# A decoder trunk on one core: the even mixer's projections in another order, ScalarE's order written out there, and the next norm finished on VectorE

## The chip, the cores and the metric

One core of one Trainium2 chip. The metric is the device time of one execution in microseconds. The kernel before has three timed runs of 955.73, 953.67 and 952.62 us; their median, 953.67 us, is what the change is held against. One further execution was profiled.

## The reference

Two layers over a sequence of 256 tokens with 1024 channels, everything in float32. Each layer is an FFN, a mixer, and another FFN, each behind an RMS norm and added to the residual x. Layer 0 has the even mixer, layer 1 the odd one. Cut to what matters:

```python
def swiglu(x, w_gate, w_up, w_down):
    return (jax.nn.silu(x @ w_gate) * (x @ w_up)) @ w_down

def even_mixer(h, ...):
    a_val, a_gate, q, k, v = jnp.split(h @ w_in, cuts, axis=-1)   # 512, 512, 512, 128, 128
    u = a_val * jax.nn.sigmoid(a_gate)
    u = causal depthwise convolution of u, 31 taps, + conv_b
    u = jax.nn.silu(layer_norm(u, ln_g, ln_b))
    q = rms_norm(q per head, q_g)        # 8 heads of 64
    k = rms_norm(k per head, k_g)        # 2 heads of 64
    o = banded_attention(q, k, v, 127, sinks)
    return concatenate([u, o]) @ w_out

x = x + 0.5 * swiglu(rms_norm(x, g[0]), ...)
x = x + mixer(rms_norm(x, g[1]))
x = x + 0.5 * swiglu(rms_norm(x, g[2]), ...)
```

## The kernel before

**Weights.** All weights pass through TensorE as two float32r parts. A *unit* (`unit`, L159) is a slab of 512 rows by 512 columns (or fewer): SyncE loads it into one of three `raw` buffers, ScalarE copies it to `hi` and VectorE writes `lo = raw - hi`, each in two pieces of 128x1024. Four pairs of `hi` and `lo` are there. `prepare(n)` (L155) makes units up to number n, and `take(ahead)` (L191) hands out the next one after it has prepared `ahead` of them. A unit's `raw` buffer comes free, and the next load starts, when its `lo` is written. `EV_CUTS` (L138) lists which columns of the even input projection stand in which unit.

**Products.** One product of activations and weights is three matmuls per chunk of 128 rows (`products`, L202): hi by hi, lo by hi, hi by lo. A projection of 128 tokens to 512 columns is two units of 12 matmuls (kh = 0 and 1); with both token halves it is 48 matmuls. `run(steps, n)` issues the next n matmuls of such a list, so that other work can be written between them. Results stand in four PSUM banks (`bank`, L58); scores and the convolution's turned results share two (`sbank`), transposes two others (`tbank`).

**Norms.** A `Norm` (L280) works on x in four parts, token half t by column half d: x is transposed on TensorE (`pt`), VectorE multiplies by the gain (`xg`), ScalarE copies it to the `hi` part of `xt`, VectorE subtracts for the `lo` part, and ScalarE squares x and sums it up (`junk`). `finish` turns the sums into 1/rms by 13 or 16 small operations (`inv_sqrt`, L240). That factor is needed only where a projection's result is read, so projections start without it. Only the norm of the even mixer (n = 1) is finished on VectorE; the others are on GpSimd.

**FFN** (L341). For six column groups: the gate's projection, silu on ScalarE (`sg`, L354, the first reader of 1/rms), the up projection, their product on VectorE (`h`), its transpose and split; then the down projection.

**Even mixer** (L528 to L699). The first convolution gate comes ahead of L530; from there on VectorE's and TensorE's orders are as written, while the scheduler still sets ScalarE's. Half of the convolution runs on VectorE (`taps`, 62 operations of `dve_tap`, L552, two channel halves), half on TensorE (`conv`, 64 matmuls `pc` with diagonal weights `wT`). The order is: first conv gate, q, k and v, second conv gate. Then `attention` (L425) goes through eight heads with a lag: `sc` scores, a VectorE maximum with its mask, ScalarE's exponential, the transpose `pp` of the head two back, and the value products `o`. `fill(i)` puts five taps, and from the fourth step on six `conv` matmuls, between the heads. The output projection takes o first (`mixer_first`), while the convolution goes through its layer norm (`cn`, `yn`, `yt`, `utl`); `mixer_last` (L501) adds the rest, adds to x, and calls the next norm through `after`, partly behind the manual section (`todo`).

**Odd mixer** (L701) uses the same `attention` and `mixer_last`; all its engines are ordered by the scheduler.

Of the kernel before, what the change touches and what calls it, by code (L numbers as in the profile page):

```python
# [16 lines left out]
F32 = mybir.dt.float32  # L17
# [24 lines left out]
def tile_trunk(ctx: ExitStack, tc: tile.TileContext, x, norm_g, w_gate, w_up, w_down,  # L42
# [297 lines left out]

    def ffn(xp, nxt, then=None):  # L341
# [83 lines left out]
    def attention(qT, vn, kchunk, vcol, mask, first, fill, last=lambda nm: None):  # L425
# [7 lines left out]
        def scores(i):  # L433
            c, s = divmod(i, 2)
            pr, cq = slice(64 * s, 64 * s + 64), slice(c * 128, (c + 1) * 128)
            sc = sbank("sc")
            kk = kchunk(c)[pr]
            nc.tensor.matmul(sc[:, 0:256], qT[1][pr, cq], kk, start=True, stop=True)  # L438
            nc.tensor.matmul(sc[:, 256:384], qT[0][pr, cq], kk[:, 0:128], start=True, stop=True)  # L439
            p[i] = work.tile([128, 384], F32, name="p", tag="p", bufs=4)  # L440
            init = -LOW if first is None else first(c, s)
            for t, ks, m in ((1, slice(0, 256), mask), (0, slice(256, 384), mask[:, 128:256])):
                nc.vector.tensor_tensor_reduce(p[i][:, ks], sc[:, ks], m, -1.0, init, ALU.add, ALU.min,
                                               nm[:, i, t:t + 1])
            for t, ks in ((1, slice(0, 256)), (0, slice(256, 384))):
                nc.scalar.activation(p[i][:, ks], p[i][:, ks], AF.Exp, bias=nm[:, i, t:t + 1], scale=-1.0,
                                     accum_out=ls[:, i, t:t + 1])
# [53 lines left out]
    def mixer_last(ys, src, nxt):  # L501


        n = 4 // len(src[0])
        todo = []
# [22 lines left out]
    def even_mixer(xp, nxt):  # L528
        gv = project(xp, 512)
        with tc.manual_schedule(engines={mybir.EngineType.DVE, mybir.EngineType.PE}):  # L530
            todo = even_rest(xp, nxt, gv)
        run(todo)

    def even_rest(xp, nxt, gv):
# [38 lines left out]
        def gated(ps, r, dst):  # L573
# [4 lines left out]
            nc.vector.scalar_tensor_tensor(dst, v[0], r, v[1], op0=ALU.mult, op1=ALU.mult)  # L578

        u = [nat("u") for t in range(2)]  # L580
        for t in range(2):
            gated(gv[t], xp.r[t], u[t][:, :256].rearrange("p (g c) -> p g c", c=64))
        qps, steps = projects(xp, 512)
        for t in range(2):
            run(steps, 9)
# [3 lines left out]
        run(steps, 6)  # L589
        rp = xp.parities()  # L590
        run(taps, 4)
        run(steps)
        run(taps, 6)
        hs = work.tile([128, 20], F32, name="hs", tag="hs", bufs=1)
        kps, steps = projects(xp, 256)
        run(steps, 24)
        qns = [head_sums(qps[t], xp.r[t], 8, hs[:, 8 * t:8 * t + 8], "q") for t in range(2)]
        run(steps)
        run(taps, 2)
        gv, steps = projects(xp, 512, PARITY, WB - 1)  # L600
        run(steps, 8)
        kns = [head_sums(kps[t], xp.r[t], 2, hs[:, 16 + 2 * t:18 + 2 * t], "k") for t in range(2)]
# [5 lines left out]
        rh = inv_sqrt(hs, 1.0 / 64, 20)  # L608
        kT = work.tile([128, 512], F32, name="kT0", tag="kT0", bufs=1)
        qT = [slot("qT", "l") for t in range(2)]  # L610
        kns = [head_norm(kns[t], rh[:, 16 + 2 * t:18 + 2 * t], 2) for t in range(2)]
        qns = [head_norm(qns[t], rh[:, 8 * t:8 * t + 8], 8, paired=True) for t in range(2)]
        run(steps, 32)
        run(taps, 6)
        for t in range(2):
            k_to_T(kns[t], vo[:, 17:18], 1, [kT], t)
        run(steps, 2)
        for t in range(2):
            q_to_T(qns[t], gq_e, qT[t])
        run(steps)  # L620
        u2 = nat("u2").rearrange("p (g r c) -> p g r c", g=4, r=2)

        def fill(i):
            if i == 0:
                for r in range(2):
                    gated(gv[r], rp[:, r:r + 1], u2[:, :, r])
            elif i == 2:
                pt = transposed(u2.rearrange("p g r c -> p (g r c)"))
                for j in range(2):
                    nc.scalar.activation(vT[j][:, :, PADB:PADB + 128], pt[:, 2 * j:2 * j + 2], AF.Copy)  # L630
            elif i > 2:
                run(conv, 6)
            run(taps, 5)
            if i in (3, 6):
                prepare(cursor[0] + WB - 2 + i // 3)

# [40 lines left out]
        run(steps, 24)  # L677
        us = [[], []]
# [22 lines left out]
    def odd_mixer(xp, nxt):  # L701
# [51 lines left out]
        run(mixer_first(ys, us))  # L753
        run(mixer_last(ys, [[p] for p in o], nxt))

# [48 lines left out]
    for g in range(4):  # L804
        rows, c = slice(g % 2 * 64, g % 2 * 64 + 64), 2 + g // 2
        for r in range(2):
# [5 lines left out]
              (5, ffn)]  # L812
    cur = n0
    for n, f in phases:
        nxt = Norm(n + 1) if n < 5 else None
        f(cur, nxt)
        cur = nxt
# [53 lines left out]
```

## Time and profile before

| | us |
|---|---|
| median of three runs | 953.67 |
| the profiled execution, its own time | 955.37 |
| its span, first to last instruction | 953.3 |
| PE busy (98% of the span) | 938.3 |
| DVE busy (56%) | 537.9 |
| ACT busy (47%) | 451.2 |
| POOL busy (10%) | 98.9 |

PE is TensorE, DVE VectorE, ACT ScalarE, POOL GpSimd, SP SyncE's queue of transfers. PEclk is the clock granted to TensorE as a share of full speed: 1.00 is 2.4 GHz, 0.50 is 1.2 GHz. Busy time counts a matmul as busy at either clock, so a slow stretch doesn't show as idle. In a row of the timeline the first number is the start in us from the span's beginning, the second the busy time of the whole row, "x12" the number of recorded instructions (a plain float32 matmul leaves two records), and what stands in brackets is the idle time ahead of it and who ended it.

### The profile page before, as it was taken

How to read it: one execution, taken by the hardware profiler on the slowest of the kernel's cores; microseconds unless marked ns; L12 is line 12 of the kernel's file. 1: busy time of each engine (PE TensorE's matmuls, PEld its weight loads, DVE VectorE, ACT ScalarE, POOL GpSimd, SP SyncE). 2: the span in 40 equal slices, each digit the busy share in tenths (PEclk: the TensorE clock that was granted, in tenths of full speed). 3: DMA queues.
4: the chain of work that ended last, by engine and by line, in shares of the span. 5: the costliest groups of instructions: out<-in, count | busy, mean ns of one | idle time of the engine just before them, and what ended most of it. 6: DMA issues, size and time to landing. Idle time of an engine off the chain costs nothing.

```text
span 953.3 us, 11336 instructions
## 1 busy us (share of the span) xinstructions
PE 938.3 (98%) x4431; PEld 777.9 (82%) x4431; DVE 537.9 (56%) x748; ACT 451.2 (47%) x654; POOL 98.9 (10%) x142
## 2 busy tenths in 40 slices
PE   7999999999999899999999999999999999999998
PEld 6888887878897688888778888888788888888876
DVE  6855464669964575554555555545662285555551
ACT  6644454356445254444454444443567464443430
POOL 3000000720000300000002000000253260000000
PEclk9999999999799999999999999999999999999999
DMA  8855545547112565555565555456654066655640
GB/s 299 289 191 184 183 164 188 186 144 189 65 45 89 177 225 194 174 180 181 186 207 177 180 190 182 160 206 203 216 177 133 7 230 208 191 182 177 193 140 23
DMA packets 91975, 164.75 MB, mean 173 GB/s; under 512 B 3825, under 2 KB 17969, under 8 KB 91921
## 3 DMA queue, kind: packets, MB, share of 16 engines
q1 hardware_dynamic: 91120, 163.07, 52.3%
q0 software_dynamic: 736, 0.93, 0.4%
q8 instruction: 35, 0.57, 0.3%
q14 instruction: 20, 0.16, 0.1%
q10 hardware_dynamic: 64, 0.02, 0.0%
HBM read 162.96 MB, written 1.05 MB: 172 GB/s over the span
## 4 chain that ended last, share of the span: by engine, by line
PE 84%; issue 12%; POOL 2%; DMA 1%; ACT 0%; DVE 0%; POOLq 0%
PE pj L334 53%; PE y L200 24%; PE pt L237 3%; PE m L334 1%; PE m L200 1%; POOL wT L547 1%; DMA sink_b<-in_ev_sinks_dram 1%; PE sc L438 0%; PE pp L452 0%; POOL na L250 0%; PE o L460 0%; PE o L459 0%; PE pp L738 0%; PE p L743 0%; PE sc L439 0%
## 5 line engine op out<-in xcount | busy, mean ns | idle before, releaser
L331 DVE TENSOR_TENSOR lo<-raw,hi 128x1024 fp32r<-128x1024 f32 (+2 forms) x306 | 358.3, 1208 | 228.8 <-ACT hi L331 221.9
L331 ACT ACTIVATE hi<-raw 128x1024 fp32r<-128x1024 f32 (+3 forms) x311 | 308.5, 1039 | 322.5 <-PE pj L334 149.3
L334 PE MATMUL pj<-hi,xt 128*128 128x512 f32 (+2 forms) x1664 | 412.8, 388 | 3.7 <-ACT sg L354 3.1
L334 PEld LDWEIGHTS pj<-hi,xt 128*128 128x128 f32 x1664 | 309.6, 189 | 64.6 <-ACT sg L354 3.5
L334 PE MATMUL pj<-lo,xt 128*128 128x512 f32 (+2 forms) x832 | 225.1, 387 | 0.0
L334 PEld LDWEIGHTS pj<-lo,xt 128*128 128x128 f32 x832 | 154.8, 188 | 28.2
L200 PE MATMUL y<-hi,hth 128*128 128x512 f32 x352 | 138.6, 394 | 0.0
L200 PE MATMUL y<-hi,htl 128*128 128x512 f32 x336 | 131.6, 392 | 0.0
L200 PE MATMUL y<-lo,hth 128*128 128x512 f32 x352 | 100.9, 397 | 0.0
L200 PEld LDWEIGHTS y<-lo,hth 128*128 128x128 f32 x352 | 65.4, 188 | 18.3 <-issue 5.6
L200 PEld LDWEIGHTS y<-hi,hth 128*128 128x128 f32 x352 | 66.1, 188 | 16.0 <-issue 2.9
L200 PEld LDWEIGHTS y<-hi,htl 128*128 128x128 f32 x336 | 63.1, 188 | 12.7
L361 DVE SCALAR_TENSOR_TENSOR h<-pj,nr,sg 128x512 f32<-128x512 f32 (+1 forms) x48 | 33.3, 693 | 38.4 <-PE pj L334 38.3
L331 ACT ACTIVATE hth<-pt 128x512 fp32r<-128x512 f32 x40 | 23.8, 595 | 56.0 <-PE pt L237 56.0
L331 DVE TENSOR_TENSOR htl<-pt,hth 128x512 fp32r<-128x512 f32 x40 | 27.5, 690 | 29.9 <-ACT hth L331 29.9
L354 ACT ACTIVATE sg<-pj,nr 128x512 f32<-128x512 f32 (+1 forms) x48 | 30.4, 634 | 28.9 <-PE pj L334 24.3
L276 POOL TENSOR_TENSOR s<-ss 128x2 f32<-128x2 f32 x4 | 2.9, 718 | 324.9 <-ACT junk L271 324.9
L331 DVE TENSOR_TENSOR xg<-pt,g_n 128x512 f32<-128x512 f32 x24 | 16.5, 688 | 22.8 <-PE pt L237 22.8
L237 PE MATMUL pt<-ident,h 128*128 128x128 f32 x176 | 27.6, 272 | 0.0
L331 POOL TENSOR_TENSOR lo<-raw,hi 128x2048 fp32r<-128x2048 f32 x5 | 23.4, 4687 | 35.6 <-ACT hi L331 35.6
L237 PEld LDWEIGHTS pt<-ident,h 128*128 128x128 f32 x176 | 22.1, 140 | 5.4
L556 DVE SCALAR_TENSOR_TENSOR acc<-uT,cw,acc 128x256 f32<-128x256 f32 x60 | 24.8, 479 | 0.0
(184 smaller groups left out, 552.8 us busy)
## 6 DMA issues: line engine op xcount, KB each, us to landing
raw<-in_ffn_w_up_dram SPq DMA_DIRECT2D x40, 1024.0 KB, 5.2
raw<-in_ffn_w_down_dram SPq DMA_DIRECT2D x40, 1024.0 KB, 5.0
raw<-in_ffn_w_gate_dram SPq DMA_DIRECT2D x38, 1024.0 KB, 5.1
raw<-in_od_w_in_dram SPq DMA_DIRECT2D x8, 1024.0 KB, 5.0
raw<-in_ev_w_in_dram SPq DMA_DIRECT2D x10, 512.0 KB, 4.1
raw<-in_od_w_out_dram SPq DMA_DIRECT2D x4, 1024.0 KB, 5.0
raw<-in_ffn_w_gate_dram SPq DMA_DIRECT2D x8, 384.0 KB, 3.5
raw<-in_ffn_w_up_dram SPq DMA_DIRECT2D x8, 384.0 KB, 4.2
```

The lines of the kernel that those rows point to most:

```text
L200: f()
L237: nc.tensor.transpose(ps[:, j * 128:(j + 1) * 128], src[:, j * 128:(j + 1) * 128], ident)
L276: eng.tensor_tensor(s2, sv[:, :, 0], sv[:, :, 1], op=ALU.add)
L331: steps.pop(0)()
L334: f()
L354: nc.scalar.activation(s[:, :n], gs[t], AF.Silu, scale=xp.r[t])
L361: nc.vector.scalar_tensor_tensor(h[:, :n], us[t] if fg == 5 else us[t][:, :], xp.r[t], sg[t][:, :n], op0=ALU.mult, op1=ALU.mult)
L547: nc.gpsimd.tensor_tensor(w, eye2.unsqueeze(1).to_broadcast([128, 8, 64]), taps2[:, g, 8 * h:8 * h + 8].unsqueeze(2).to_broadcast([128, 8, ...
L556: nc.vector.scalar_tensor_tensor(acc[c], src, w, acc[c], op0=ALU.mult, op1=ALU.add)
```

## The change

It has five parts.

1. `EV_CUTS`: the third and fourth entry change places. The second conv gate is projected third, k and v last.
2. The even mixer's manual section takes ScalarE in, and `even_rest` is written anew: splits at chosen places (`split_next`), taps spread over the projections, q's and k's norms apart (two `inv_sqrt`, of 16 and of 4 columns, where one of 20 stood), the table of the exponential loaded ahead (`warm`), 16 conv matmuls ahead of k's transposes and three behind them, and in the attention three conv matmuls and three taps per head.
3. `attention`: the exponentials are issued behind the turn and the values of the same step.
4. `mixer_last`: the next norm's parts are issued by column halves inside the section, the next FFN's first gate projection (`head`) is written there too, and 1/rms is finished on VectorE (`nxt.finish(nc.vector)`) ahead of the splits that follow. This holds for both mixers; two chains of 16 operations leave GpSimd and two of 13 come to VectorE.
5. `ffn` takes a finished first gate projection as `head`.

The matmuls and transposes are the same 4,275, the transfers the same 207 in the same order on SP's queue (two of them now bring other columns).

```diff
-    EV_CUTS = (((512, 256), (0, 256)), ((1024, 512),), ((1536, 256),), ((768, 256), (256, 256)))
+    EV_CUTS = (((512, 256), (0, 256)), ((1024, 512),), ((768, 256), (256, 256)), ((1536, 256),))
...
-                g = project(xp, 512)
+                g = head if fg == 0 and head else project(xp, 512)
...
+            if i < 8:
+                exps(i)
             fill(i)
...
         for d in range(2):
-            hi, lo = take(WB - 1)
-            for t in range(2):
-                for j, (h, l) in enumerate(src[t]):
-                    ks = slice(n * j, n * j + n)
-                    product(ys[t][d], h, l, hi[:, ks], lo[:, ks], 512, FULL[:n], False, j == len(src[t]) - 1)
-                run(todo)
+            w = take(WB - 1)
+            for t in range(2):
+                steps = last(d, t, *w)
+                if d == 1:
+                    run(steps, 6)
+                    nxt.part(t, 0)
+                run(steps)
                 nc.vector.tensor_tensor(xs[t][d], ys[t][d], xs[t][d], op=ALU.add)
-                todo.append(partial(after, nxt, t, d))
-            prepare(cursor[0] + WB - 1)
-        return todo
+            if d == 0:
+                prepare(cursor[0] + WB - 1)
+        ps, steps = projects(nxt, 512, HALVES, WB - 1)
+        for t in range(2):
+            run(steps, 12)
+            nxt.part(t, 1)
+        nxt.finish(nc.vector)
+        prepare(cursor[0] + WB)
+        run(steps)
+        return ps
...
-        with tc.manual_schedule(engines={mybir.EngineType.DVE, mybir.EngineType.PE}):
-            todo = even_rest(xp, nxt, gv)
-        run(todo)
+        with tc.manual_schedule(engines={mybir.EngineType.DVE, mybir.EngineType.PE, mybir.EngineType.Activation}):
+            return even_rest(xp, nxt, gv)
...
+        gv, steps = projects(xp, 512, PARITY, WB - 1)
+        run(steps, 1)
...
+        warm(AF.Exp, u2[:, 0, 0, 0:1])
+        kps, steps = projects(xp, 256, HALVES, WB - 1)
...
+        run(conv, 16)
         kT = work.tile([128, 512], F32, name="kT0", tag="kT0", bufs=1)
-        for t in range(2):
-            k_to_T(kns[t], vo[:, 17:18], 1, [kT], t)
+        for t in range(2):
+            k_to_T(kns[t], vo[:, 17:18], 1, [kT], t)
+        run(conv, 3)
         run(taps, 6)
...
         def fill(i):
-            if i == 0:
-                for r in range(2):
-                    gated(gv[r], rp[:, r:r + 1], u2[:, :, r])
...
-            elif i > 2:
-                run(conv, 6)
-            run(taps, 5)
...
+            run(conv, 3)
+            run(taps, 3 if i < 8 else 20 - 2 * i)
...
+        o = attention_out(os_, ls, lambda t: run(conv, 4), lambda: run(conv, 8))
         run(taps)
-        o = attention_out(os_, ls, lambda t: run(conv, 4), lambda: run(conv, 8))
         run(conv)
...
-        steps = mixer_first(ys, o, WB - 1)
-        run(steps, 4)
+        steps = mixer_first(ys, o, WB - 2)
+        run(steps, 16)
```

How the built program's order moves, at the three places that the prediction speaks of. In its names `pj` is a projection's bank, `x_80` to `x_83` are the four parts of x with `x_83` the last one, and a line's number belongs to the kernel that the row is of.

TensorE at the start of the even attention, before:

```order
L237 MATMUL pk<-ident,k 128x128 x2
L334 MATMUL pj_1875<-hi,xt 128x512 x2
L237 MATMUL pq<-ident,qn 128x128 x8
L334 MATMUL pj_1875<-hi,xt 128x512 x2
L334 MATMUL pj_1875<-lo,xt 128x512 x4
L438 MATMUL sc<-kT_1914,qT 128x256
L439 MATMUL sc<-kT_1914,qT 128x128
L438 MATMUL sc<-kT_1914,qT 128x256
L439 MATMUL sc<-kT_1914,qT 128x128
L438 MATMUL sc<-kT_1914,qT 128x256
L439 MATMUL sc<-kT_1914,qT 128x128
L452 MATMUL pp<-ident,p 128x128 x3
```

and in the changed kernel:

```order
L334 MATMUL pc<-vT,wT 128x128 x16
L237 MATMUL pk<-ident,k 128x128 x2
L334 MATMUL pc<-vT,wT 128x128 x3
L439 MATMUL sc<-kT_2041,qT 128x256
L440 MATMUL sc<-kT_2041,qT 128x128
L334 MATMUL pc<-vT,wT 128x128 x3
L439 MATMUL sc<-kT_2041,qT 128x256
L440 MATMUL sc<-kT_2041,qT 128x128
L334 MATMUL pc<-vT,wT 128x128 x3
L439 MATMUL sc<-kT_2041,qT 128x256
L440 MATMUL sc<-kT_2041,qT 128x128
L455 MATMUL pp<-ident,p 128x128 x3
```

The three pairs of scores that stood one behind the other now have three convolution matmuls between them, and the last projection, which stood ahead of the scores, has moved ahead of k's.

VectorE and ScalarE behind the even mixer's last residual add (`x_83`), before, VectorE first:

```order
L513 TENSOR_TENSOR x_83<-m_2314,x_83 128x512
L331 TENSOR_TENSOR lo<-raw,hi 128x1024 x6
L331 TENSOR_TENSOR xg<-pt,g_n 128x512
L331 TENSOR_TENSOR lo<-raw,hi 128x1024 x2
L331 TENSOR_TENSOR xt<-xg,xt 128x4x128
L361 SCALAR_TENSOR_TENSOR h<-pj_2642,nr,sg 128x512
```

```order
L271 ACTIVATE junk,ss<-x_83 128x512
L331 ACTIVATE hi<-raw 128x1024 x2
L354 ACTIVATE sg<-pj_2572,nr 128x512
L331 ACTIVATE xt<-xg 128x4x128
L331 ACTIVATE hi<-raw 128x1024 x2
L354 ACTIVATE sg<-pj_2573,nr 128x512
```

and in the changed kernel:

```order
L524 TENSOR_TENSOR x_83<-m_2317,x_83 128x512
L331 TENSOR_TENSOR lo<-raw,hi 128x1024 x2
L331 TENSOR_TENSOR xg<-pt,g_n 128x512
L331 TENSOR_TENSOR xt<-xg,xt 128x4x128
L331 TENSOR_TENSOR xg<-pt,g_n 128x512
L331 TENSOR_TENSOR xt<-xg,xt 128x4x128
L276 TENSOR_TENSOR s_2594<-ss 128x2
L244 TENSOR_SCALAR nv<-s_2594 128x2
```

```order
L331 ACTIVATE xt<-xg 128x4x128
L271 ACTIVATE junk,ss<-x_83 128x512
L331 ACTIVATE hi<-raw 128x1024 x6
L355 ACTIVATE sg<-pj_2537,nr 128x512
L355 ACTIVATE sg<-pj_2538,nr 128x512
```

The chain of 1/rms, which was not on VectorE, follows the norm's parts there (eleven more of its small operations come behind the last row, then six splits `lo`); on ScalarE six splits `hi` stand between the last square (`junk`) and the first gate (`sg`), where two stood.

VectorE ahead of the even mixer, where the FFN's last residual add is done and the first conv gate's projection waits for `xt`, before:

```order
L331 TENSOR_TENSOR xg<-pt,g_n 128x512 x2
L331 TENSOR_TENSOR lo<-raw,hi 128x2x256 x2
L331 TENSOR_TENSOR xt<-xg,xt 128x4x128
L276 TENSOR_TENSOR s_1561<-ss 128x2
```

and in the changed kernel:

```order
L331 TENSOR_TENSOR xg<-pt,g_n 128x512 x2
L331 TENSOR_TENSOR lo<-raw,hi 128x1024 x2
L331 TENSOR_TENSOR xt<-xg,xt 128x4x128
L276 TENSOR_TENSOR s_1561<-ss 128x2
```

The unit that is split there is now the second conv gate's (512 columns) and no longer k's and v's (256).

## Rows read from the trace of the kernel before

**Rows 1.** Waits of PE: who for whom, us in total, times, longest.
```profile
PE pj L334 <- ACT sg L354: 3.1, 1, 3.1
PE pp L452 <- ACT p L446: 1.1, 1, 1.1
PE sc L438 <- DVE nm L443: 0.8, 1, 0.8
PE pj L334 <- DVE xt L331: 0.2, 1, 0.2
PE pj L334 <- ACT xt L331: 0.2, 1, 0.2
```

**Rows 2.** Windows: length, busy PE, PEld, DVE, ACT, POOL, PEclk, DMA share, GB/s.
```profile
245.00:250.00 5.00, 5.00 (x22) 4.59 (x22) 5.00 (x17) 2.35 (x9) 0.00 (x0) 0.50 0.01 3
...
770.00:800.00 30.00, 29.98 (x136) 24.50 (x135) 19.26 (x20) 15.40 (x20) 7.54 (x17) 1.00 0.64 215
```

**Rows 3.** Timeline of PE in the even attention: start, busy us, instruction, [idle before].
```profile
237.20 0.71 PE L438 MATMUL sc<-kT,qT 64*128 64x256 f32 x4
...
238.97 0.70 PE L438 MATMUL sc<-kT,qT 64*128 64x256 f32 x2 [0.84 <-DVE nm L443]
...
240.96 0.90 PE L452 MATMUL pp<-ident,p 128*128 128x128 f32 x3 [1.07 <-ACT p L446]
...
242.64 1.22 PE L438 MATMUL sc<-kT,qT 64*128 64x256 f32 x2
...
254.75 0.69 PE L438 MATMUL sc<-kT,qT 64*128 64x256 f32 x2
...
258.08 0.70 PE L438 MATMUL sc<-kT,qT 64*128 64x256 f32 x2
```

**Rows 4.** Timeline of PE, gate and up products behind the even mixer.
```profile
316.39 1.98 PE L334 MATMUL pj<-hi,xt 128*128 128x512 f32 x8
...
322.37 3.65 PE L334 MATMUL pj<-hi,xt 128*128 128x512 f32 x8 [3.10 <-ACT sg L354]
```

**Rows 5.** Timeline of DVE behind the even mixer: residual add, splits.
```profile
309.50 0.68 DVE L513 TENSOR_TENSOR x<-m,x 128x512 f32<-128x512 f32 x1
310.10 6.89 DVE L331 TENSOR_TENSOR lo<-raw,hi 128x1024 fp32r<-128x1024 f32 x6
```

**Rows 6.** Timeline of POOL there: first and last of its 16 operations.
```profile
311.08 0.29 POOL L276 TENSOR_TENSOR s<-ss 128x2 f32<-128x2 f32 x1 [113.94 <-ACT junk L271]
...
321.39 0.20 POOL L255 TENSOR_TENSOR nr<-nr,na 128x2 f32<-128x2 f32 x1
```

**Rows 7.** Timeline of ACT there: a split that waits for its weights.
```profile
317.78 2.00 ACT L331 ACTIVATE hi<-raw 128x1024 fp32r<-128x1024 f32 x2 [6.78 <-DMA raw<-in_ffn_w_gate_dram]
```

**Rows 8.** Timeline of DVE ahead of the even mixer: split, xt, rstd chain's ends.
```profile
202.26 1.28 DVE L331 TENSOR_TENSOR lo<-raw,hi 128x512 fp32r<-128x512 f32 x2
203.46 0.68 DVE L331 TENSOR_TENSOR xt<-xg,xt 128x512 fp32r<-128x512 f32 x1
...
204.74 0.16 DVE L244 TENSOR_SCALAR nv<-s 128x2 f32<-128x2 f32 x1
...
206.77 0.16 DVE L252 SCALAR_TENSOR_TENSOR nr<-na,nr 128x2 f32<-128x2 f32 x1
```

**Rows 9.** Timeline of PE at the end of the even attention.
```profile
269.95 3.35 PE L334 MATMUL pc<-vT,wT 128*128 128x128 f32 x28
...
273.13 1.04 PE L237 MATMUL pt<-ident,on 128*128 128x128 f32 x8
...
276.72 0.63 PE L661 MATMUL cn<-ident,acc 128*128 128x128 f32 x4
```

**Rows 10.** Timeline of DVE: taps, split of o, last step of the layer norm.
```profile
217.97 2.46 DVE L556 SCALAR_TENSOR_TENSOR acc<-uT,cw,acc 128x256 f32<-128x256 f32 x6
...
274.46 1.29 DVE L331 TENSOR_TENSOR otl<-pt,oth 128x512 fp32r<-128x512 f32 x2 [3.03 <-ACT oth L331]
...
281.64 1.90 DVE L675 TENSOR_SCALAR yn<-cn,mv,nr 128x256 f32<-128x256 f32 x4
```

More of the change, by code (lines that the diff above doesn't have):

```diff
@@ L339, in warm, with ffn @@
         nc.scalar.activation(t, src, func)
-    def ffn(xp, nxt, then=None):
+    def ffn(xp, nxt, then=None, head=None):
         hts = [[None, None] for _ in range(6)]
@@ L504, in mixer_last, with last @@
         n = 4 // len(src[0])
[L505 removed]
+        def last(d, t, hi, lo):
+            for j, (h, l) in enumerate(src[t]):
+                ks = slice(n * j, n * j + n)
+                yield from products(ys[t][d], h, l, hi[:, ks], lo[:, ks], 512, FULL[:n], False, j == len(src[t]) - 1)
         for d in range(2):
[L507 removed]
+            w = take(WB - 1)
             for t in range(2):
[L509 to L516 removed]
+                steps = last(d, t, *w)
[3 more added lines that the diff above has]
+                run(steps)
+                nc.vector.tensor_tensor(xs[t][d], ys[t][d], xs[t][d], op=ALU.add)
+            if d == 0:
[8 more added lines that the diff above has]
+        return ps
     def q_to_T(qn, gain, dst):
@@ L578, in gated, with split_next @@
             nc.vector.scalar_tensor_tensor(dst, v[0], r, v[1], op0=ALU.mult, op1=ALU.mult)
+        def split_next():
+            prepare(cursor[0] + WB - 1)
         u = [nat("u") for t in range(2)]
@@ L582, in even_rest @@
             gated(gv[t], xp.r[t], u[t][:, :256].rearrange("p (g c) -> p g c", c=64))
-        qps, steps = projects(xp, 512)
+        qps, steps = projects(xp, 512, HALVES, WB - 1)
         for t in range(2):
-            run(steps, 9)
+            run(steps, 10 - 2 * t)
             pt = transposed(u[t], 2)
@@ L588, in even_rest @@
                 nc.scalar.activation(uT[c][:, PAD + t * 128:PAD + (t + 1) * 128], pt[:, c], AF.Copy)
-        run(steps, 6)
         rp = xp.parities()
+        split_next()
+        run(taps, 6)
+        run(steps, 18)
+        split_next()
+        run(taps, 8)
+        run(steps)
+        gv, steps = projects(xp, 512, PARITY, WB - 1)
+        run(steps, 1)
+        hs = [work.tile([128, n], F32, name="hs", tag=f"hs{n}", bufs=1) for n in (16, 4)]
+        qns = [head_sums(qps[t], xp.r[t], 8, hs[0][:, 8 * t:8 * t + 8], "q") for t in range(2)]
+        run(steps, 11)
+        split_next()
+        rh = inv_sqrt(hs[0], 1.0 / 64, 16)
+        qns = [head_norm(qns[t], rh[:, 8 * t:8 * t + 8], 8, paired=True) for t in range(2)]
+        run(steps, 13)
         run(taps, 4)
         run(steps)
-        run(taps, 6)
-        hs = work.tile([128, 20], F32, name="hs", tag="hs", bufs=1)
-        kps, steps = projects(xp, 256)
-        run(steps, 24)
-        qns = [head_sums(qps[t], xp.r[t], 8, hs[:, 8 * t:8 * t + 8], "q") for t in range(2)]
-        run(steps)
[L599 to L602, printed above, removed]
+        split_next()
+        u2 = nat("u2").rearrange("p (g r c) -> p g r c", g=4, r=2)
+        for r in range(2):
+            gated(gv[r], rp[:, r:r + 1], u2[:, :, r])
+        warm(AF.Exp, u2[:, 0, 0, 0:1])
+        kps, steps = projects(xp, 256, HALVES, WB - 1)
+        run(steps, 24)
+        split_next()
+        run(steps, 18)
+        qT = [slot("qT", "l") for t in range(2)]
+        pt = transposed(u2.rearrange("p g r c -> p (g r c)"))
+        for j in range(2):
+            nc.scalar.activation(vT[j][:, :, PADB:PADB + 128], pt[:, 2 * j:2 * j + 2], AF.Copy)
+        run(steps)
+        kns = [head_sums(kps[t], xp.r[t], 2, hs[1][:, 2 * t:2 * t + 2], "k") for t in range(2)]
+        for t in range(2):
+            q_to_T(qns[t], gq_e, qT[t])
+        rh = inv_sqrt(hs[1], 1.0 / 64, 4)
+        kns = [head_norm(kns[t], rh[:, 2 * t:2 * t + 2], 2) for t in range(2)]
         vn = []
@@ L607, in even_rest @@
             vn.append(v)
-        rh = inv_sqrt(hs, 1.0 / 64, 20)
+        run(conv, 16)
         kT = work.tile([128, 512], F32, name="kT0", tag="kT0", bufs=1)
[L610 to L614, printed above, removed]
         for t in range(2):
             k_to_T(kns[t], vo[:, 17:18], 1, [kT], t)
-        run(steps, 2)
-        for t in range(2):
-            q_to_T(qns[t], gq_e, qT[t])
-        run(steps)
-        u2 = nat("u2").rearrange("p (g r c) -> p g r c", g=4, r=2)
-        def fill(i):
-            if i == 0:
-                for r in range(2):
-                    gated(gv[r], rp[:, r:r + 1], u2[:, :, r])
[L627 to L630, printed above, removed]
-            elif i > 2:
-                run(conv, 6)
-            run(taps, 5)
-            if i in (3, 6):
-                prepare(cursor[0] + WB - 2 + i // 3)
+        run(conv, 3)
+        run(taps, 6)
+        def fill(i):
+            run(conv, 3)
+            run(taps, 3 if i < 8 else 20 - 2 * i)
         es = work.tile([128, 8, 2], F32, name="es", tag="es", bufs=1)
@@ L676, in even_rest @@
                                         op0=ALU.subtract, op1=ALU.mult)
-        run(steps, 24)
+        run(steps, 20)
         us = [[], []]
@@ L753, in odd_mixer @@
         run(mixer_first(ys, us))
-        run(mixer_last(ys, [[p] for p in o], nxt))
+        return mixer_last(ys, [[p] for p in o], nxt)
     n0 = Norm(0)
@@ L812, in tile_trunk @@
               (5, ffn)]
-    cur = n0
+    cur, head = n0, None
     for n, f in phases:
         nxt = Norm(n + 1) if n < 5 else None
-        f(cur, nxt)
+        head = f(cur, nxt, head=head) if n in (2, 5) else f(cur, nxt)
         cur = nxt
```

1 line of the change is left out of this document (added).

## The prediction

> **What bounds the kernel now.** I read the waits first. TensorE is busy for 938.3 of 953.3 us, so only two things can be won: the time in which it waits, and the time in which it runs slowly. Besides the first load, which the change leaves alone, five waits have a name [rows 1]: 3.1 us for a gate's `sg`, 1.1 and 0.8 us in the even attention, and twice 0.2 us for `xt`. The reader is to see that all five lie in or right behind the even mixer. The table of windows comes second, because a slow clock doesn't show as idle: around 245 us TensorE is busy for all of 5 us, but at a granted clock of 0.50, that is at 1.2 GHz instead of 2.4 [rows 2]. Behind the odd mixer, where the change also reaches, it is busy for 29.98 of 30 us at full clock [rows 2]: nothing can be won there.
>
> The timeline then prices both. In the attention the third pair of scores comes 0.84 us late and the first transposes of p 1.07 us late [rows 3]. Until then the clock was full; from about 241 us it is half. One step of a head (a pair of scores, `pp`, `o`, six conv matmuls) takes 254.75 to 258.08, 3.33 us, at full clock; the two steps before it take 242.64 to 254.75, 12.11 us [rows 3]. Behind the mixer the eight products after the 3.1 us wait take 3.65 us, where eight take 1.98 at full clock [rows 4].
>
> **The change part by part, first what it removes.** *Attention.* Both waits come from VectorE: between the first two heads' maxima it does two gates and five taps. The second gate has moved ahead of the attention, and a step holds three taps of 0.41 us (2.46 for six [rows 10]) instead of five. TensorE's step shrinks by three conv matmuls of 0.23 us (14 from 269.95 to 273.13 [rows 9]), so VectorE's share falls by 0.82 us and TensorE's step by 0.69: in the later steps, which wait for nothing now, nothing gets tighter, and the first steps gain fillers that they did not have. I take both waits as gone, 1.91 us. With them I take the slow clock as gone: from 240.96 to 254.75 are 13.79 us at a rate of 6.66 to 12.11, or 0.55, so 6.2 us are lost there. Against this stands a small loss: before, the first two pairs of scores follow each other at once and take 237.20 to 238.13 together, no longer than the one pair from 238.97 to 239.89 [rows 3]. With conv matmuls between them they no longer share that time: 0.9 us. Attention in all: 1.9 + 6.2 - 0.9 = 7.2 us.
>
> *The seam to the next FFN.* The wait for `sg` is a wait for 1/rms. The last residual add is at 309.50; POOL's 16 operations then take 311.08 to 321.59 beside six splits on VectorE [rows 5, 6]; TensorE has run out of other products at 319.27. In the change, from the add on, VectorE does it (0.7), one pair of splits (2.3: six take 6.89 [rows 5]), two parts of the norm with ScalarE's copy between (about 2.0 each, from 0.7 us operations), and the chain (2.2: 204.74 to 206.93 for its last twelve [rows 8]): 9 us. ScalarE adds six splits of 1.0 us [rows 7] behind its last square, so `sg` can start some 13 us after the add. TensorE's order has 96 products of about 0.23 us, 22 us, ahead of the next one that needs the gate's bank. The wait is gone with 9 us to spare, and so are the 1.67 us of slow clock behind it and the two waits of 0.2: 3.1 + 1.7 + 0.4 = 5.2 us.
>
> Next to it stands a rule of the Trainium skill, page "TensorE: Matmul & The Clock Gate", section "Architectural detail": ScalarE's queue is a strict first in, first out. ScalarE's 6.78 us in front of a split whose weights had not landed [rows 7], with `sg` next in its order, fit it. By the rule a late load would hold `sg` behind six splits now, and the sum would lose what the third rival prices; by the rows it loses 0.
>
> In the odd mixer the same chain comes to VectorE, 2.2 us; it is busy for 19.26 of 30 us there [rows 2] and TensorE waits for none of it, so 0 (2.2 if that cover were gone). SP's transfers keep their order. A load starts when VectorE has written a `lo`; at this seam two splits come earlier than before and six later, with a DMA share of 0.64 [rows 2]: 0.
>
> **What it adds.** Each is a wait that the trace of before doesn't have, so each has two ends.
> - Ahead of the mixer, the pair of splits in front of `xt` is now of the large kind: 2.30 instead of 1.20 us [rows 5, 8]. TensorE did not wait at that place, and one more product of 0.23 us stands ahead of it. Between 0 and 1.1; as the old margin can't be seen I take 0.8, nearer the upper end, because `xt` starts with no idle time behind the splits.
> - k's transposes and the copies to `kT` now stand three conv matmuls ahead of the first scores. Between 0 and the 0.84 of rows 3; I take 0.1, since 16 conv matmuls (3.7 us) cover k's norm.
> - The layer norm's first transposes `cn` wait for the last eight taps, which moved behind o's split: 2.62 us from `pt` to the end of the split [rows 9, 10], and 3.3 for the taps, 5.9. TensorE's cover is 0.9 for `pt`, 0.9 for four conv matmuls and 16 products, 3.7 to 4.0: 5.5 to 5.8. Between 0 and 0.4; I take 0.3.
> - From `cn` to the first two `yn` are 276.72 to 282.6 [rows 9, 10], 5.9 us; the cover now is `cn` itself (0.8) and 20 products (4.6). Between 0 and the 1.3 that would be left if `cn` covered nothing; I take 0.5.
> - The first `utl` stands behind a pair of weight splits, 2.3 us, at most that; most lies under 12 products and four transposes, and I take 0.2.
>
> Sum: 12.4 won, 1.9 lost, 10.5 us net; with the ends, 6.5 to 12.4. The profiled execution's own time is 955.37 (span 953.3), so its like would be 944.9; it stands 1.7 us above the median of 953.67, so for the median I say **943.2 us**, and 941.3 to 947.2 by the ends.
>
> **Rivals.**
> 1. *The clock falls all the same, for a while.* The stretch of small matmuls is now one piece, with no projection in it, and the margins at its start are short. It would cost what it costs now, 6.2 us: 949.4. For it: the fall of before came after waits of only about 1 us each. Against it: the waits that came first are the ones taken out.
> 2. *Slower: the clock falls at the start of that stretch and does not come back until the output projection.* The stretch is 64 conv matmuls (14.7 us), eight steps without theirs (3.33 - 1.4 = 1.95 each, 15.6) and the transposes at its ends (2): 32 us. At 0.55 it takes 58, so 26 us more: 969. It decides from the point where the slow stretch lasts longer than 10.5 / 0.45 = 23 us. Against it: from 254.75 to the end of the attention the same kinds ran for 18 us at the full rate [rows 3, 9], and the clock had come back among them.
> 3. *`sg` is held up on ScalarE behind a late load.* Before, the load that was late let ScalarE start 317.78, 8.3 us after the add [rows 5, 7]. With six splits behind that, `sg` starts at 14.3 us; TensorE needs it at 22. Only with 12 us of lateness on top would it cost 4 us: 947. VectorE frees two buffers before the add now, which speaks against it.
> 4. *What is won is given back.* TensorE reaches the FFN 10 us earlier, and weights could become the bound. It would end near 952. Against it: a DMA share of 0.64 and VectorE two thirds busy at the seam [rows 2].
>
> **How the numbers follow.** The forecast has 0.70; the first rival 0.13, the second 0.05, the third 0.05, the fourth 0.05, and 0.02 is for a gain above the ends. A measurement of this kernel can tell about 0.3% from no change, 2.9 us. Faster by more than that: 0.70 + 0.13 + 0.05 + 0.02 = 0.90. Within it: the fourth rival, 0.05. Slower: the second, 0.05. The range takes in the forecast's ends with 1 us for the scatter of the runs (952.62 to 955.73) and reaches up to the first rival: 940.3 to 949.9. It leaves out the second and the fourth rival and the 0.02.
>
> **What would show it.** Right: no wait for `sg`, `pp` or `sc` among TensorE's waits; PEclk of 1.00 in every window from the mixer's start to the next FFN; POOL without the two chains; new waits of TensorE of under 1 us each, for `xt`, `cn` and `yt`; the mixer with its seam shorter by about 10 us, and the rest of the span as it was. Wrong: a window of 0.5 clock anywhere in the attention, a wait of some us for a weight split or for `sg` in the FFN behind it, or a second attention that lost time because its exponentials are issued later.

## The result, and the profile after

The changed kernel takes **943.98 us** (median of four runs, 942.83 to 946.36) against 953.14 for the kernel before in the same comparison: a ratio of 0.9902, 95% interval 0.9875 to 0.993, so 7 to 12 us faster. The forecast was 943.2. The profiled run took 944.27, its span is 942.4, where that of before was 953.3.

TensorE's waits in the profile after (who for whom, us in total, times, longest):

```profile
PE ps_g_n L90 <- DMA ident<-in_ident_dram: 5.6, 1, 5.6
PE pt L237 <- DVE xg L331: 0.7, 1, 0.7
PE pj L334 <- DVE xt L331: 0.5, 1, 0.5
```

None of the five waits of before [rows 1] is left. The first two rows here belong to the first load, which the change leaves alone; the third is the new wait for `xt` ahead of the even mixer. The same two windows as in [rows 2] (length, busy PE, PEld, DVE, ACT, POOL, PEclk, DMA share, GB/s):

```profile
245.00:250.00 5.00, 5.00 (x32) 4.11 (x32) 5.00 (x19) 3.33 (x13) 0.00 (x0) 1.00 0.00 0
770.00:800.00 30.00, 30.00 (x138) 24.82 (x137) 17.62 (x17) 14.52 (x18) 0.00 (x0) 1.00 0.66 216
```

In the attention the granted clock is now 1.00 where it was 0.50; behind the odd mixer GpSimd's chain is gone and TensorE is as busy as before. To see where the time went, three marks of TensorE's timeline serve: the first down-projection product `y` of the FFN ahead of the even mixer, the output projection's first `m`, and the next FFN's first `y` (the last two `y` below open the down projections of the two FFNs around the odd mixer). The trace of before:

```profile
133.31 0.39 PE L200 MATMUL y<-hi,hth 128*128 128x512 f32 x1
...
275.71 0.48 PE L334 MATMUL m<-hi,oth 128*128 128x512 f32 x1
...
429.69 0.39 PE L200 MATMUL y<-hi,hth 128*128 128x512 f32 x1
...
614.53 0.39 PE L200 MATMUL y<-hi,hth 128*128 128x512 f32 x1
...
888.57 0.39 PE L200 MATMUL y<-hi,hth 128*128 128x512 f32 x1
```

and after:

```profile
134.29 0.39 PE L200 MATMUL y<-hi,hth 128*128 128x512 f32 x1
...
270.34 0.47 PE L334 MATMUL m<-hi,oth 128*128 128x512 f32 x1
...
418.84 0.39 PE L200 MATMUL y<-hi,hth 128*128 128x512 f32 x1
...
603.64 0.39 PE L200 MATMUL y<-hi,hth 128*128 128x512 f32 x1
...
877.68 0.39 PE L200 MATMUL y<-hi,hth 128*128 128x512 f32 x1
```

From `y` to `y` the even mixer took 296.38 us and takes 284.55, 11.83 less: 6.35 of it up to the first `m` (142.40 to 136.05, "the front"), 5.48 behind it (153.98 to 148.50, "the seam"). The next stretch, which has no mixer, is 184.80 where it was 184.84; the last one, with the odd mixer, is 274.04 in both. These marks are used for all runs below; they leave out the first load, whose end wanders by some 3 us from run to run (`y` at 132.7 to 135.8).

At the seam, VectorE and then ScalarE after the change, as [rows 5 to 7] show them before:

```profile
298.22 0.68 DVE L524 TENSOR_TENSOR x<-m,x 128x512 f32<-128x512 f32 x1
...
307.67 0.16 DVE L252 SCALAR_TENSOR_TENSOR nr<-na,nr 128x2 f32<-128x2 f32 x1
307.75 6.90 DVE L331 TENSOR_TENSOR lo<-raw,hi 128x1024 fp32r<-128x1024 f32 x6
```

```profile
305.30 5.79 ACT L331 ACTIVATE hi<-raw 128x1024 fp32r<-128x1024 f32 x6
310.99 0.67 ACT L355 ACTIVATE sg<-pj,nr 128x512 f32<-128x512 f32 x1
```

1/rms is there 9.6 us after the last residual add, the gate 12.8 us after it; TensorE meanwhile has products and waits for neither.

### The profile page after: what moved, and what is told of

The parts are those of the page before. It is cut to its first block, busy times and chain, and to the rows that moved or that the text cites. A ratio compares the mean times of both kernels' runs of the same rounds, so it can differ in the third digit from the quotient of the medians.

```text
span 942.4 us, 11337 instructions
## 1 busy us (share of the span) xinstructions
PE 931.9 (99%) x4431; PEld 772.4 (82%) x4431; DVE 543.6 (58%) x786; ACT 450.9 (48%) x655; POOL 82.2 (9%) x110
## 4 chain that ended last, share of the span: by engine, by line
PE 98%; DVE 1%; DMA 1%; issue 0%; ACT 0%; POOL 0%; DVEq 0%; POOLq 0%
PE pj L334 59%; PE y L200 26%; PE m L334 4%; PE pt L237 3%; PE pc L334 2%; PE sc L439 1%; PE pp L455 1%; DMA sink_b<-in_ev_sinks_dram 1%; PE o L463 0%; PE o L462 0%; PE sc L440 0%; PE o L461 0%; DVE lo L331 0%; PE pq L237 0%; PE p L769 0%
```

## The experiments

**What makes the first waits of the attention?** The prediction said VectorE's taps and gates.

Fewer taps, in the kernel before:

```diff
-            run(taps, 5)
+            run(taps, 2 if i < 3 else 5)
```

> The kernel before, with two taps instead of five in each of the first three attention steps of the even mixer (the rest run at the end, as they did). The stage is read from the even mixer's first projection to the next FFN's first down-projection product: 228.0 us before. Theory (VectorE's queue ahead of the maxima makes TensorE wait, and these two waits bring the clock down): the waits for the third scores (0.84) and the first transposes of p (1.07) are gone or under 0.3 each, no window of the attention below a granted clock of 0.9, and the stage is shorter by 5 to 8 us (220 to 223). Rival A (the clock falls because of the small matmuls themselves): the waits go, the clock still falls to 0.5, the stage gains 2 us at most. Rival B (the gates, not the taps, hold the maxima): the waits stay over 0.6, nothing is gained.

Measured: 954.36 us against 954.38, ratio 0.9998 (0.9986 to 1.001). TensorE's timeline has both waits to the hundredth:

```profile
240.62 0.70 PE L438 MATMUL sc<-kT,qT 64*128 64x256 f32 x2 [0.84 <-DVE nm L443]
...
242.60 0.71 PE L452 MATMUL pp<-ident,p 128*128 128x128 f32 x3 [1.07 <-ACT p L446]
```

So the prediction's reason fell: the taps don't hold these two. The front is 139.88 here, 2.5 less than in the profile of before, but the kernel below that only changes the engine of 1/rms, and leaves the attention as it was, has 139.90: the slow stretch is of uneven length by itself. By the granted clock it lasts some 14 us in the profile of before and some 7 in these two. ScalarE's timeline in the kernel before shows what stands in front of `p`:

```profile
236.62 2.00 ACT L331 ACTIVATE hi<-raw 128x1024 fp32r<-128x1024 f32 x2
238.51 0.48 ACT L576 ACTIVATE sg<-pj,rp 128x256 f32<-128x256 f32 x1
239.01 1.28 ACT L446 ACT_TABLE_LOAD   x1
240.30 0.51 ACT L446 ACTIVATE p<-p,nm 128x256 f32<-128x256 f32 x1
```

A split, the second gate and the load of Exp's table follow each other without a gap, while the first maxima were ready at 238.9. VectorE's timeline there shows that it wasn't late for these maxima either; it stood idle for 0.85 us until the scores came:

```profile
238.15 0.48 DVE L443 CUSTOM_DVE_ANT_0 p<-sc,m_even,sink_n 128x256 f32<-128x256 f32 x1 [0.85 <-PE sc L439]
```

The third pair of scores needs the bank that these maxima free. So the first wait would be the way from the scores through the maxima, and the second ScalarE's. The next three kernels test that.

No conv matmuls in the first four attention steps, in the changed kernel:

```diff
-            run(conv, 3)
+            run(conv, 0 if i < 4 else 3)
```

> The changed kernel without conv matmuls in the first four attention steps; these twelve run behind the attention. New theory, after the runs with fewer taps: the first wait of before is the scores' own way (two banks for scores, so the third pair waits until the first head's maxima have read theirs; the taps do not count), and TensorE needs something else to do there. Then the third scores wait 0.6 to 0.9 us and the fourth up to 0.6; p is in time, since the table of Exp is loaded early. If short waits alone pull the clock down, a window at 0.5 follows and 4 to 8 us are lost; if it takes both waits of before, the clock stays full and 0 to 1.5 us are lost. Rival (the prediction's: VectorE's queue, which is shorter now): no wait over 0.3 at the scores, no loss.

Measured: the wait of 0.84 is back, with the gates long done and three taps a step, and no wait for `p`:

```profile
245.82 0.70 PE L439 MATMUL sc<-kT,qT 64*128 64x256 f32 x2 [0.84 <-DVE nm L444]
...
247.68 0.70 PE L439 MATMUL sc<-kT,qT 64*128 64x256 f32 x2 [0.47 <-DVE nm L444]
```

So the first wait is the scores' own way through their two banks, and the conv matmuls fill it. The clock fell in a part of the runs only: six of the ten took 941.91 to 945.57 us at a mean granted clock of 1.0, four took 948.55 to 955.61 at 0.987 to 0.992. Median 945.0. The trace is of one of the six; that the four had the same waits is assumed.

The same without the early load of Exp's table:

```diff
-            run(conv, 3)
+            run(conv, 0 if i < 4 else 3)
...
-        warm(AF.Exp, u2[:, 0, 0, 0:1])
```

> The same with Exp's table not loaded ahead of the attention, so that the load of 1.28 us stands in front of the first exponential, as it did before the change. New theory: the second wait of before (the first transposes of p, 1.07) is ScalarE's: a weight split, a gate and this load stand in front of the exponential. Then the first transposes of p wait 0.8 to 1.5 us here and not in the run without conv matmuls alone, and the clock falls to 0.5 for 8 to 14 us: 5 to 8 us lost against the changed kernel. Rival (the gates on VectorE held the maxima): no wait for p, the same time as without conv matmuls alone.

Measured: 944.98 us, waits of 0.84 and 0.47 as before, none for `p`, mean clock 1.0 in all four runs. That expectation failed: the load starts right behind k's copy at 244.47, ends at 245.8, and the first exponential at 246.0 waits for VectorE's maxima last. The table alone was not the cause.

The split out of ScalarE's way, in the kernel before:

```diff
-        kps, steps = projects(xp, 256)
+        kps, steps = projects(xp, 256, HALVES, WB - 1)
...
-        gv, steps = projects(xp, 512, PARITY, WB - 1)
+        gv, steps = projects(xp, 512, PARITY, WB - 2)
```

> The kernel before, with the weights of k's and the gates' projections split one slab later, so that ScalarE's order no longer has a weight split (2.0 us) ahead of the second gate and the first exponential of the even attention. Theory (p was late because of ScalarE's queue: a split, the gate, the table): the first exponential starts about 239.1 on the old clock instead of 240.3, the wait for p falls from 1.07 to under 0.3 us, that for the third scores stays at 0.84. If both waits are needed for the clock to fall, it stays full in most runs and up to 6 us are gained; if the one suffices, under 2 us. Rival (it was VectorE's maxima): the wait for p stays over 0.8.

Measured: 955.05 us, ratio 1.002 (1.0008 to 1.0032), slower by a little. The first exponential starts 1.89 us behind the first scores where it was 3.10, and the wait of 1.07 for the first `p` is gone, so the split was its cause. But other waits come in its place; TensorE's timeline, then VectorE's:

```profile
240.67 0.64 PE L452 MATMUL pp<-ident,p 128*128 128x128 f32 x3
...
243.26 0.70 PE L438 MATMUL sc<-kT,qT 64*128 64x256 f32 x2 [1.51 <-DVE nm L443]
...
244.68 0.86 PE L452 MATMUL pp<-ident,p 128*128 128x128 f32 x3 [0.50 <-ACT p L446]
...
266.36 0.71 PE L452 MATMUL pp<-ident,p 128*128 128x128 f32 x3 [1.52 <-ACT p L446]
```

```profile
239.69 0.87 DVE L578 SCALAR_TENSOR_TENSOR u<-pj,rp,sg 128x256 f32<-128x256 f32 x2
240.48 2.06 DVE L556 SCALAR_TENSOR_TENSOR acc<-uT,cw,acc 128x256 f32<-128x256 f32 x5
242.45 0.47 DVE L443 CUSTOM_DVE_ANT_0 p<-sc,m_even,sink_n 128x256 f32<-128x256 f32 x1
...
262.93 2.34 DVE L331 TENSOR_TENSOR lo<-raw,hi 128x1024 fp32r<-128x1024 f32 x2
```

With ScalarE out of the way it is VectorE's gates and taps, the prediction's reason, that hold the second head's maxima, and they cost 1.51. Near the end of the attention a pair of weight splits on VectorE stands ahead of the last maxima, and TensorE waits another 1.52 for `p`. The first three limits lie behind one another: the banks, ScalarE's queue, VectorE's queue. Taking one away shows the next; neither single edit of the kernel before gained anything. The clock did not follow the waits here: after 0.85, 1.51 and 0.50 us of them it was at half for some 3 us only.

**Do waits bring the clock down?** More waits, in the changed kernel:

```diff
-            run(conv, 3)
-            run(taps, 3 if i < 8 else 20 - 2 * i)
+            run(conv, 0 if i < 4 else 3)
+            run(taps, 5 if i < 8 else 20 - 2 * i)
```

> The changed kernel without conv matmuls in the first four attention steps, and with five taps in a step instead of three. VectorE then has 0.68 of maxima and 2.06 of taps, 2.7 us per head, where TensorE has 1.95: four waits of 0.6 to 0.9 us in a row for the scores. Theory (short waits among small matmuls bring the clock down, and more of them do so more surely; without conv matmuls and with three taps the time had two levels, 944 and 949 to 956): the clock falls in most runs, the profile has windows at 0.5 for 8 to 14 us, 5 to 9 us lost against the changed kernel. Rival (the two levels had another cause): clock at 1.0, only the waits, 2 to 3 us lost.

Measured: 954.84 us, 10.9 above the changed kernel's median, where 5 to 9 were expected; mean clock 0.985 to 0.994 in all ten runs. There are two waits, not four, 0.84 and 1.26, and the clock falls during the second. TensorE's order is that of the kernel without conv matmuls; only VectorE has more taps. Windows of TensorE (columns as above):

```profile
245.00:250.00 5.00, 3.74 (x16) 3.09 (x14) 5.00 (x18) 2.61 (x10) 0.00 (x0) 0.57 0.00 0
250.00:255.00 5.00, 5.00 (x21) 4.37 (x20) 5.00 (x18) 2.53 (x10) 0.00 (x0) 0.50 0.00 0
...
265.00:270.00 5.00, 5.00 (x21) 4.59 (x22) 2.04 (x8) 1.36 (x5) 0.00 (x0) 0.50 0.00 0
270.00:275.00 5.00, 5.00 (x34) 5.00 (x33) 0.43 (x2) 2.00 (x4) 0.00 (x0) 0.70 0.02 3
```

At 1.2 GHz TensorE is then busy without a gap and stays slow for some 27 us by the windows from 245 to 275. From the first scores to `m` are 40.15 us; the kernel without conv matmuls has 26.97 there with 1.31 of waits, so 0.8 of the 13.2 more are waits and 12.4 the clock. The whole gain of the change is gone, with 2.1 us of waits.

**What is the seam worth, and through what?** The even mixer's end as it was, in the changed kernel (`mixer_last_old` is the function of before):

```diff
-            return even_rest(xp, nxt, gv)
+            todo = even_rest(xp, nxt, gv)
+        run(todo)
...
-        return mixer_last(ys, us, nxt)
+        return mixer_last_old(ys, us, nxt)
```

> The changed kernel with the even mixer's end as it was: residual adds, splits and 1/rms behind the output projection, 1/rms on GpSimd, no projection of the next FFN ahead of it. Attention and projections as changed. Theory (the seam is worth 5 to 6 us by itself, 3.1 of it the wait for the gate, 1.7 the clock behind it): a wait of 2.5 to 3.5 us for sg behind the mixer, a window at a lower clock right after it, and a stage of 221 to 222.5 us where it is 216.2 in the changed kernel. Rival (the attention's full clock makes the seam's wait shorter, or the splits come in other places): a wait under 1.5 us and a stage below 219.

Measured: 947.11 us (945.76 to 950.05), 3.1 above the changed kernel's median; in the profile, which is the run of 950.05, the seam takes 153.64, 5.1 more. So the seam is worth 3 to 5 us, a little under the theory. The wait that was expected did not come: there is none for `sg`, but these,

```profile
PE pj L334 <- ACT xt L331: 1.4, 1, 1.4
PE pt L237 <- DVE xg L331: 1.4, 1, 1.4
PE pt L237 <- DVE x L548: 1.2, 1, 1.2
```

of which the second is the first load's. After them the clock falls too, to 0.76 from 305 to 310 us and 0.90 from 310 to 315. The old end costs time in these surroundings as well, but through `xt` and the residual add; that the wait for `sg` is what was taken out is not shown by this run.

Only the engine of 1/rms, in the kernel before:

```diff
-                nxt.finish(nc.vector if nxt.n == 1 else nc.gpsimd)
+                nxt.finish(nc.vector if nxt.n in (1, 2) else nc.gpsimd)
```

> The kernel before, with 1/rms behind the even mixer on VectorE and nothing else changed; VectorE's order then has it behind six weight splits and among two more. Theory (the gain of the seam is the place ahead of the splits, not the engine): 1/rms ends about 323 us where it ended at 321.6, the wait for sg is 3 to 5 us, and the time is the same as before within 0.3%. Rival (the engine is the gain): 1/rms ends by 319, the wait for sg falls below 1 us, and 3 to 5 us are gained.

Measured: 952.63 us, ratio 0.9982 (0.9964 to 1.0): 1.8 us, and at most 3.4, of the seam's 5; in the profile the seam takes 151.40, 2.6 less than before. The time is as expected, the waits are not: 1/rms ends later (14.2 us after the add, 12.1 before), yet there is no wait for `sg`, but two of 1.08 and 0.94 for `xt`, whose part of the norm still stands behind six splits on VectorE and here behind a late one on ScalarE:

```profile
314.86 2.01 ACT L331 ACTIVATE hi<-raw 128x1024 fp32r<-128x1024 f32 x2 [6.79 <-DMA raw<-in_ffn_w_gate_dram]
...
316.77 0.61 ACT L331 ACTIVATE xt<-xg 128x512 fp32r<-128x512 f32 x1
```

The rule of a strict first in, first out (the Trainium skill, "TensorE: Matmul & The Clock Gate", "Architectural detail") agrees: `xg` was ready at 314.66 and `xt` waited 2.1 us behind a split that it doesn't need.

The new place on the old engine, in the changed kernel:

```diff
-        nxt.finish(nc.vector)
+        nxt.finish(nc.gpsimd)
```

> The changed kernel with 1/rms at the end of both mixers on GpSimd again, in the new place. Theory (what counts is that TensorE has 96 products, 22 us, ahead of the gate): the 16 operations take 4 to 11 us on GpSimd, end some 18 us after the last add, TensorE waits less than 0.3 us for sg, and the time is the changed kernel's within 0.3%. Rival (VectorE's chain itself carries the gain): a wait of 2 us or more for sg behind a mixer, with a lower clock behind it, 3 to 5 us lost.

Measured: 944.29 us, seam 148.51 where it was 148.50, no wait for `sg`. In the new place the engine counts for nothing; what counts is the place, with the products that TensorE has in between. GpSimd's timeline, with VectorE's six splits behind it:

```profile
306.61 0.19 POOL L276 TENSOR_TENSOR s<-ss 128x2 f32<-128x2 f32 x1 [107.34 <-ACT junk L271]
...
307.64 1.16 POOL L249 TENSOR_TENSOR na<-ny 128x2 f32<-128x2 f32 x1
...
313.42 1.06 POOL L250 TENSOR_TENSOR na<-na,nv 128x2 f32<-128x2 f32 x1
...
315.98 0.20 POOL L255 TENSOR_TENSOR nr<-nr,na 128x2 f32<-128x2 f32 x1
```

```profile
307.52 6.91 DVE L331 TENSOR_TENSOR lo<-raw,hi 128x1024 fp32r<-128x1024 f32 x6 [0.87 <-ACT hi L331]
```

**Small parts.** The split ahead of `xt` later, in the changed kernel:

```diff
-        gv = project(xp, 512)
+        gv, steps = projects(xp, 512, HALVES, WB - 1)
+        run(steps)
```

> The changed kernel with the weight splits ahead of the even mixer's first projection put off by one slab, so that VectorE comes to xt sooner. Theory (the new wait of 0.5 us for xt, 0.8 with what it stretches, is due to the larger pair of splits ahead of it): no wait for xt at that place, 0.5 to 0.9 us gained, which five rounds can just tell. Rival (the load or ScalarE comes last): the wait stays, or comes back in the next projection.

Measured: 944.92 us, the same; the wait for `xt` is gone, one of 0.5 comes at the next place (`rT`, for `uT` on ScalarE, behind the split), and the stretch from `y` to `y` is 284.26, 0.3 less. The rival was right.

ScalarE's order left to the scheduler, in the changed kernel:

```diff
-        with tc.manual_schedule(engines={mybir.EngineType.DVE, mybir.EngineType.PE, mybir.EngineType.Activation}):
+        with tc.manual_schedule(engines={mybir.EngineType.DVE, mybir.EngineType.PE}):
```

> The changed kernel with ScalarE's order in the even mixer left to the scheduler, as it was before; it has all exponentials in much the same order but weight splits earlier, one between q's and k's copies. Theory (ScalarE has 1.5 to 1.9 us free there, so its fixed order is worth nothing by itself): no wait over 0.3 us beyond those of the changed kernel, the same time within 1.5 us. Rival (a split in front of k's copy or of an exponential makes TensorE wait as before): 0.5 to 2 us of waits for kT, sc or p, and a lower clock in part of the runs.

Measured: 944.67 us, the same within what can be told; a wait of 0.7 for `vT` at q's transposes, which the theory did not have, and 285.75 from `y` to `y`, 1.2 more. By the profile the fixed order is worth about 1 us; the medians, 0.7 apart, can't tell it from nothing.

**A version that beats both.** The scores of two heads back to back, in the changed kernel:

```diff
-            if i < 8:
+            if i < 8 and not pairs:
                 scores(i)
+            elif i < 8 and i % 2 == 0:
+                scores(i)
+                scores(i + 1)
```

> The changed kernel with the scores of two heads issued back to back in the even attention, the rest in order. The two heads stand on different halves of the rows, and before the change two pairs of scores took 0.93 us together where one takes 0.92. Theory (the halves work side by side): four times up to 0.9 us gained, 2.5 to 3.7 us, the step of two heads 4.5 instead of 5.3 us. Rival (two banks: the next pair of heads waits for the maxima of both): a wait of 0.5 us or more at each pair, nothing gained, or a fallen clock and 4 to 6 us lost.

Measured: 940.71 us (940.05 to 940.89), ratio to before 0.986 (0.9845 to 0.9875), 3.3 us under the changed kernel's median; the front is 132.13, 3.92 less. Two heads take 4.39 us, from 250.18 to 254.57,

```profile
250.18 0.76 PE L439 MATMUL sc<-kT,qT 64*128 64x256 f32 x4
...
254.57 0.71 PE L439 MATMUL sc<-kT,qT 64*128 64x256 f32 x4
```

where the changed kernel takes 2.67 for one, 5.33 for two:

```profile
251.63 0.70 PE L439 MATMUL sc<-kT,qT 64*128 64x256 f32 x2
...
254.30 0.70 PE L439 MATMUL sc<-kT,qT 64*128 64x256 f32 x2
```

The 0.94 us that are saved are about one pair of scores (0.92). By the Trainium skill ("TensorEngine Tiling (Array Packing)", "Theoretical Speedup") two products over at most 64 rows can run at up to twice the rate; the trace agrees: two heads' scores take 0.93 us where one head's take 0.92 [rows 3].

All three edits together (pairs, later split, four taps in steps three to seven):

> The changed kernel with the scores in pairs, the split in front of the even mixer's first projection put off by one slab, and four taps instead of three in the attention steps three to seven. Theory: the pairs bring 3.9 us as they did alone, the split 0.3, the earlier taps 0.2 to 0.5 at the waits for cn and yt (stage from the first m product to the next FFN's first down-projection 148.5 before, 148.0 to 148.3 here): a time of 939.8 to 940.4. Rival (the attention is shorter, so VectorE's four taps per step now hold the maxima): waits at the scores of 0.3 us or more, nothing beyond the pairs' 3.9.

Measured: 939.82 us, ratio 0.9857 (0.9842 to 0.9873), not to be told from the pairs alone. From `y` to `y` are 280.63, with the pairs alone 280.62: the seam gains 0.4, the split 0.25, and the attention gives 0.7 back, without a wait that the trace names.

## Why the prediction was right, and where its reasons were not

- **The attention's 7.2 us.** The front is 6.35 shorter although it carries two of the new waits (0.83 for `xt`, 0.08 for `kT`): 7.3 won. The size was right. The step that failed is "Both waits come from VectorE": the third scores waited for the way through two banks, `p` for a split on ScalarE; VectorE was the third limit, hidden behind the second. The change removes all three (conv matmuls between the scores, the gate early, three taps), so the sum held in spite of the reason, which is luck. The prediction did say that the first steps gain fillers, and the run without them shows that this is what counts. What remains uneven is the slow stretch: kernels with the same two waits had fronts of 142.40, 139.88 and 139.90, so the profile of before was one of the slower cases. Its mean clock says the same: 0.991, where only four of the nineteen runs of that kernel beside the one with fewer taps had 0.991 or less, and those four took 955.32 to 957.61 us. For the usual run the 6.2 us of slow clock were thus too large by some 2.5, an estimate from these fronts: 11.83 from `y` to `y` less 2.5 makes 9.3, and the medians differ by 9.2. The forecast took the full gain of the slow profile off the median; that it came out near, because the seam gave more than its term, is luck as well.
- **The slow clock goes with the waits.** Right, and now shown by adding waits under the same order of TensorE: with two of 2.1 us together it falls in ten runs of ten, with two of 1.3 in four of fourteen (the two kernels without conv matmuls at the start), and in none of the changed kernel's four, which has none there. The price of the second rival, 0.45 us for each slow one, held: some 27 slow us cost 12.4, 0.46 each. That rival is nearer than its 0.05 suggests: in that kernel two waits of about 1 us at the start of the stretch did half of it. How long the clock stays down is not priced by the waits: some 3 us in the kernel with the split put off, some 7 or 14 with the waits of before, some 27 here.
- **The seam's 5.2 us** was undersized. The seam is 5.48 shorter and carries 0.17 for `otl`, 0.17 for `cn`, 0.45 for `yt` and 0.04 for `utl`: 6.3 won. Before, from 286 to 330 us, TensorE was idle for 3.6 us and lost 1.7 to the clock; another 0.9 never showed as idle: eight products from 297.24 took 2.20 to the next one where eight from 303.56 took 1.81, and around the two waits of 0.2 another 0.5 went the same way. The two rows of 0.2 [rows 1] were taken at their face. The mechanism was right: 9 us and 13 us after the add were forecast for 1/rms and the gate, 9.6 and 12.8 came. That VectorE does it was no part of it. The wait itself is not as sure as the time: with only the engine changed, or with the old end in the changed kernel, there was no wait for `sg` either, and time went through `xt` instead. The row of [rows 7], which the prediction set beside the Trainium skill's rule on ScalarE's queue, can't bear that rule out, because up to 317.59 nothing behind that split was ready (`xg` of the next `xt` ends there, 1/rms at 321.59); the 2.1 us of `xt` behind a split, in the kernel with only the engine changed, can.
- **The costs of 1.9** came to 1.7: `xt` 0.83 (forecast 0.8), `kT` 0.08 (0.1), `cn` 0.17 (0.3), `yt` 0.45 (0.5), `utl` 0.04 (0.2), and 0.17 for `otl`, which the sum did not have. Rows of the changed kernel for three of them (seven products stand behind `xt`'s wait; a `yt` without a wait takes 0.60):

```profile
206.24 1.90 PE L334 MATMUL pj<-hi,xt 128*128 128x512 f32 x7 [0.48 <-DVE xt L331]
...
274.32 0.80 PE L687 MATMUL cn<-ident,acc 128*128 128x128 f32 x4
...
280.11 0.91 PE L709 MATMUL yt<-ident,yn 128*128 128x128 f32 x4
...
282.23 0.60 PE L709 MATMUL yt<-ident,yn 128*128 128x128 f32 x4
```

- **The odd mixer, the DMA, the third and fourth rival: 0.** Right: no stretch behind the even mixer's FFN changed by more than 0.04 us.

Left open: what decides, in the kernel with 1.3 us of waits, in which runs the clock falls (only runs at full clock left a trace), and what sets how long it stays down.

## What to carry to other kernels

The engine named in a wait can be the last of several that are late: before an edit is priced, read what the others would have held up, and expect that removing one limit shows the next. Short waits can cost far more than their length where small matmuls follow, so give TensorE independent products at the start of such a stretch; and where two products use different halves of the rows, issue them back to back.

## What the runs showed of the hardware

- TensorE's clock fell to 0.50 with two waits of 0.84 and 1.26 us among small matmuls, and stayed there for some 27 us, in which TensorE was busy without a gap from 246.4 us on. With waits of 0.85, 1.51 and 0.50 us in another kernel it stayed there for some 3 us.
- GpSimd's operations on 128x2, in the kernel with 1/rms on GpSimd in the new place, took 1.03 to 1.16 us while VectorE ran its six splits (307.5 to 314.4) and 0.19 to 0.22 ahead of and behind them.
- Two score products on different halves of the rows take the time of one: 0.93 us for two heads, 0.92 for one, in the kernel before.
